# Attention without a division of the probabilities: the inverse sums go through memory and scale the values

## The chip, the core and the metric

The program runs on one core of a Trainium2 chip. Its engines work side by side, each through its own list in order: TensorE (PE in the profile, with PEld for its weight loads), VectorE (DVE), ScalarE (ACT), GpSimd (POOL) and SyncE (SP), which here only issues transfers. The metric is the device time of one execution in microseconds (us); lower is better.

## What is computed

A trunk of two layers over 512 positions of width 1024. Layer 0 mixes positions with a state-space scan and has a gated feed-forward part; layer 1 is attention over 16 heads, then a second feed-forward part. The change touches only the attention:

```python
s = jnp.einsum('bhqd,bhkd->bhqk', q_blk, k).astype(jnp.float32) * scale
s = jnp.where(key_pos[None, :] <= query_pos[:, None], s, NEG_INF)
p = jax.nn.softmax(s, axis=-1).astype(v.dtype)
return jnp.einsum('bhqk,bhkd->bhqd', p, v)
```

Each head has keys and queries of 96 and values of 64 numbers per position. The softmax divides each row of exp(s - max) by its sum; since that divisor belongs to a query, it can be applied to the row of probabilities, or later to the 64 values that come out for this query.

## The kernel before, in words

The kernel is written in a framework that takes the operations in program order, with their dependences and buffers, and works out by an estimate of its own the order of each engine's list. So an edit in one place can shift the order all around it. A tile name has a fixed number of buffers (`bufs`); who needs a buffer waits until its last reader is done.

Attention works on heads one by one (`for h in range(H)`), in four quarters of four heads. A quarter is opened (its three weight slabs are loaded by SP, split into a high part `wh` on ScalarE and a low part `wl` on VectorE, lines 141 and 142), its queries and keys are projected block by block, and it is closed (`close_q`, `close_k`): root mean squares by some 25 small VectorE operations (the tiles `r41...` and `r42...`), then the queries `Qt` and the keys `Kt` are scaled on VectorE and GpSimd. Quarters are projected ahead of their heads, so that three closings fall between the heads of earlier quarters.

For a head, `scores(h)` makes four blocks of rows of the score matrix in a PSUM bank (block i has 128 queries and (i + 1) * 128 keys), takes each row's negative maximum (line 968, VectorE), and makes `p = exp(s - max)` with its row sum `sm` on ScalarE (line 970). Line 971 inverts the sum on VectorE (one number per partition), and line 973 multiplies the block by it, on VectorE for block 3 and on GpSimd for blocks 0 to 2. `turn_p` transposes the blocks on TensorE into `pt` (line 982). For each pair of heads, `values` multiplies `pt` by the values `Vt` into one bank `ps_po` (line 1002): head h in partitions 0 to 63, head h + 1 in 64 to 127, the queries along the row. The bank is split into a high part `oh` (ScalarE, line 168) and a low part `ol` (VectorE, line 169), while the order of positions in the row is changed. Eight such pairs feed the output projection with the slabs `w_o`, three matmuls per product; one of its eight blocks of columns (`ps_w`) is worked into the attention from head 9 on, and parts of two more are placed among the last heads.

All transfers of the attention are issued by SP, one list in order: an issue that waits for a buffer or for data holds back all issues behind it.

Of the kernel before, what the change touches and what calls it, by code (L numbers as in the profile page):

```python
# [7 lines left out]
F32 = mybir.dt.float32  # L8
# [8 lines left out]
P = 128  # L17
D = 1024
S = 512
# [3 lines left out]
T = 4  # L23
# [55 lines left out]
def places(z):  # L79

    return z.rearrange("p (i c) -> p i c", i=T)


def by_place(z):

    return z.rearrange("p (c i) -> p i c", i=T)


class Trunk:
# [779 lines left out]
    def attention(self, low, krot, tabs, tf, tfs, maskb, identb):  # L869
        tc, nc, a = self.tc, self.nc, self.a  # L870
        v, g = nc.vector, nc.gpsimd
        M_, A_, S_ = ALU.mult, ALU.add, ALU.subtract
        ident = self.c("ident")

        def tt(out, x, y, op, eng=v):
            eng.tensor_tensor(out=out, in0=x, in1=y, op=op)

        qp = self.qp
        os = []
        quarters, heads, outs = {}, {}, {}  # L880
# [74 lines left out]
        def scores(h):  # L955
            qT, kT = heads[h, "q"], heads[h, "k"]
            mx = qp.tile([P, 4], F32, name="mx")
            sm = qp.tile([P, 4], F32, name="sm")
            pbs = [None] * 4
            b2 = self.ps("s")  # L960
            for i in (0, 2, 1, 3):
                n = (i + 1) * P
                bank = b2 if i in (0, 2) else self.ps("s")
                ps = bank[:, 384:512] if i == 0 else bank[:, 0:n]
                nc.tensor.matmul(out=ps, lhsT=qT[:, i * P:n], rhs=kT[:, 0:n], start=True, stop=False)  # L965
                nc.tensor.matmul(out=ps[:, i * P:n], lhsT=identb, rhs=maskb, start=False, stop=True)  # L966
                m1, s1 = mx[:, i:i + 1], sm[:, i:i + 1]
                v.reduce_max(out=m1, in_=ps, axis=AX.X, negate=True)  # L968
                pb = qp.tile([P, n], F32, name=f"p{i}")
                nc.scalar.activation(out=pb, in_=ps, func=AF.Exp, bias=m1, accum_out=s1)  # L970
                v.reciprocal(out=s1, in_=s1)  # L971
                eng = v if i == 3 else g
                eng.tensor_scalar(out=pb, in0=pb, scalar1=s1, scalar2=None, op0=M_)  # L973
                pbs[i] = pb
            heads[h, "p"] = pbs

        def turn_p(h, kbs, eng):
            bank = self.ps("a")
            at = 0
            for kb in kbs:  # L980
                for i in range(kb, 4):
                    nc.tensor.transpose(out=bank[:, at + (i - kb) * P:at + (i - kb + 1) * P], in_=heads[h, "p"][i][:, kb * P:(kb + 1) * P],
                                        identity=ident)
                at += S - kb * P
            pt = qp.tile([P, at], F32, name=f"pt{kbs[0]}", bufs=4)
            if eng is v:
                v.tensor_copy(out=pt, in_=bank[:, 0:at])
            else:
                nc.scalar.activation(out=pt, in_=bank[:, 0:at], func=AF.Copy)
            at = 0  # L990
            for kb in kbs:
                heads[h, "t", kb] = pt[:, at:at + S - kb * P]
                at += S - kb * P

        def values(h):

            Vt = quarters[h // 4][4]
            po = self.ps("po")
            with tc.high_priority():
                for kb in range(4):  # L1000
                    for e in (1, 0):
                        nc.tensor.matmul(out=po[64 * e:64 * e + 64, kb * P:], lhsT=Vt[:, kb, (h + e) % 4, :], rhs=heads[h + e, "t", kb],  # L1002
                                         start=kb == 0, stop=kb == 3)
            os.append(self.pair(h // 2, "o"))
            self.split(*[y.rearrange("p (i c) -> p c i", i=T) for y in os[-1]], po.rearrange("p (c i) -> p c i", i=T))

        open_quarter(0)
        for b in range(4):
# [9 lines left out]
        for h in range(2):  # L1018
            turn(h, "q")
            turn(h, "k")  # L1020
        scores(0)
        for h in range(H):
            nq, nb = divmod(h + 7, 4)
            if h + 1 < H:
                scores(h + 1)
# [13 lines left out]
            if h % 2 == 0 and h:  # L1039
                values(h - 2)  # L1040
# [9 lines left out]
            if nq < 4:  # L1050
                proj_kv(nq, nb)
                if nb == 3:
                    close_k(nq)
        values(H - 2)
        for m in range(KD):
            w, ps = early[m] if m < 1 else (self.weights(a["w_o"][m], (KD, P), pieces=2 if m in (3, 4) else 1), self.ps(("", "s", "s", "a", "a", "a", "s", "a")[m]))
# [102 lines left out]
```

## Time and profile before

| | |
|---|---|
| median of 3 runs | 1229.52 us (1227.26 to 1230.77) |
| the profiled execution, its own time | 1228.52 us |
| its span, first to last instruction | 1226.7 us |
| mean granted clock of TensorE | 0.979 of full speed |
| TensorE busy | 1182.0 us (96% of the span) |
| VectorE, ScalarE, GpSimd busy | 664.2, 489.2, 137.2 us |
| attention, heads and closings | about 680 to 835 us from the span's start |

A view of the profile gives, for engines or groups of instructions, the busy time, the count of instructions, the mean duration of one, and what ended the idle time before them. A busy TensorE is not TensorE at its peak: its matmuls overlap, and their ends are modelled. Times in timelines and windows count from the start of the span.

### The profile page before, as it was taken

What the parts mean: (1) busy time and instruction counts of PE and PEld (TensorE: products, weight loads), DVE (VectorE), ACT (ScalarE), POOL (GpSimd) and SP (SyncE); (2) the same over time, 40 slices, a digit from 0 to 9 for tenths busy, and PEclk for the clock granted to TensorE, in tenths of its full rate; (3) what the DMA queues carried; (4) which work ended last, traced back from release to release, by engine and by line L of the source; (5) the groups of instructions that cost most, each with busy time, mean ns of one, the idle gap of its engine ahead of it and who ended that gap; (6) DMA issues with size and microseconds to landing.
All of it is one profiled execution on the core that took longest, in us unless ns stands there. A gap on an engine that the chain in (4) does not pass through costs nothing.

```text
span 1226.7 us, 15533 instructions
## 1 busy us (share of the span) xinstructions
PE 1182.0 (96%) x6133; PEld 959.8 (78%) x6136; DVE 664.2 (54%) x1194; ACT 489.2 (40%) x821; POOL 137.2 (11%) x149
## 2 busy tenths in 40 slices
PE   7977999999999999999999898999999999999998
PEld 6766777888888888888878676667888888888887
DVE  7797894357444444333358767744844444443221
ACT  7646444254232232233245766644432332322110
POOL 0300000030000000000234445432100000000000
PEclk9978799999999999999999899999999999999999
DMA  6210012323333233333222101103233232333331
GB/s 230 69 27 27 28 36 86 103 86 104 91 98 103 92 97 99 95 95 95 86 88 67 37 2 41 52 2 103 86 103 103 87 103 91 99 99 103 120 114 46
DMA packets 31896, 100.96 MB, mean 82 GB/s; under 512 B 3664, under 2 KB 4688, under 8 KB 31824
## 3 DMA queue, kind: packets, MB, share of 16 engines
q1 hardware_dynamic: 31680, 99.97, 26.2%
q8 instruction: 48, 0.79, 0.3%
q14 instruction: 24, 0.20, 0.1%
q10 hardware_dynamic: 144, 0.00, 0.0%
HBM read 97.86 MB, written 2.10 MB: 81 GB/s over the span
## 4 chain that ended last, share of the span: by engine, by line
PE 83%; DVE 9%; ACT 4%; issue 2%; POOL 1%; DMA 1%; SPq 0%; DVEq 0%; ACTq 0%
PE ps_ps L155 20%; PE ps_ps L154 20%; PE ps_ps L153 19%; PE ps_s L965 2%; PE ps_x L153 2%; PE ps_x L155 2%; PE ps_x L154 2%; PE ps_a L153 2%; PE ps_a L154 2%; PE ps_a L155 2%; DVE wl L142 1%; PE ps_x L638 1%; PE ps_g L153 1%; PE ps_x L606 1%; PE ps_po L1002 1%
## 5 line engine op out<-in xcount | busy, mean ns | idle before, releaser
L141 ACT ACTIVATE wh<-w 128x1024 fp32r<-128x1024 f32 (+3 forms) x193 | 191.3, 993 | 548.0 <-PE ps_ps L154 351.0
L142 DVE TENSOR_TENSOR wl<-w,wh 128x1024 fp32r<-128x1024 f32 (+3 forms) x193 | 221.9, 1151 | 212.8 <-ACT wh L141 212.7
L153 PE MATMUL ps_ps<-fh,wh 128*128 128x512 f32 x704 | 274.2, 390 | 0.0
L155 PE MATMUL ps_ps<-fh,wl 128*128 128x512 f32 x704 | 273.4, 389 | 0.0
L154 PE MATMUL ps_ps<-fl,wh 128*128 128x512 f32 x704 | 273.4, 389 | 0.0
L154 PEld LDWEIGHTS ps_ps<-fl,wh 128*128 128x128 f32 x704 | 132.1, 188 | 28.1 <-issue 0.5
L153 PEld LDWEIGHTS ps_ps<-fh,wh 128*128 128x128 f32 x704 | 132.1, 188 | 27.6 <-issue 0.5
L155 PEld LDWEIGHTS ps_ps<-fh,wl 128*128 128x128 f32 x704 | 132.1, 188 | 27.5
L153 PE MATMUL ps_ps<-ah,wh 128*128 128x512 f32 x352 | 136.9, 389 | 0.0
L154 PE MATMUL ps_ps<-al,wh 128*128 128x512 f32 x352 | 136.9, 389 | 0.0
L155 PE MATMUL ps_ps<-ah,wl 128*128 128x512 f32 x352 | 136.9, 389 | 0.0
L743 DVE TENSOR_TENSOR ut<-ps_ps,rstd 128x512 f32<-128x512 f32 x44 | 30.4, 691 | 127.8 <-PE ps_ps L155 127.8
L263 POOL TENSOR_TENSOR acc<-acc,sq 128x512 f32<-128x512 f32 x21 | 30.5, 1452 | 564.6 <-ACT sq L258 316.0
L153 PEld LDWEIGHTS ps_ps<-ah,wh 128*128 128x128 f32 x352 | 66.1, 188 | 13.8
L154 PEld LDWEIGHTS ps_ps<-al,wh 128*128 128x128 f32 x352 | 66.1, 188 | 13.8
L155 PEld LDWEIGHTS ps_ps<-ah,wl 128*128 128x128 f32 x352 | 66.1, 188 | 13.5
L740 DVE TENSOR_TENSOR gt<-ps_ps,rstd 128x512 f32<-128x512 f32 x44 | 30.4, 691 | 83.2 <-PE ps_ps L155 83.1
L973 POOL TENSOR_SCALAR p<-p,sm 128x128 f32<-128x128 f32 (+2 forms) x48 | 45.8, 960 | 70.6 <-DVE sm L971 59.3
L965 PE MATMUL ps_s<-kT,qT 96*128 96x384 f32 (+3 forms) x128 | 46.6, 466 | 1.5 <-ACT p L970 1.5
L970 ACT ACTIVATE p<-ps_s,mx 128x128 f32<-128x128 f32 (+3 forms) x64 | 33.4, 525 | 22.8 <-DVE mx L968 18.6
L168 ACT ACTIVATE ah<-ut 128x512 fp32r<-128x512 f32 x44 | 27.9, 634 | 30.7 <-DVE ut L744 30.7
L968 DVE TENSOR_REDUCE mx<-ps_s 128x1 f32<-128x128 f32 (+3 forms) x64 | 30.8, 486 | 15.1 <-PE ps_s L966 14.6
(384 smaller groups left out, 1756.1 us busy)
## 6 DMA issues: line engine op xcount, KB each, us to landing
w<-w_gu SPq DMA_DIRECT2D x88, 512.0 KB, 3.5
w<-w_down SPq DMA_DIRECT2D x32, 512.0 KB, 3.5
w<-w_glu SPq DMA_DIRECT2D x12, 512.0 KB, 3.5
w<-w_down SPq DMA_DIRECT2D x16, 384.0 KB, 3.1
w<-w_in SPq DMA_DIRECT2D x7, 512.0 KB, 3.6
w<-w_o SPq DMA_DIRECT2D x6, 512.0 KB, 3.2
x<-xT SPq DMA_DIRECT2D x8, 256.0 KB, 6.0
bc<-ssm_bc SPq DMA_DIRECT2D x8, 256.0 KB, 2.8
```

What stands on the lines that cost most here:

```text
L141: nc.scalar.activation(out=wh[:, c], in_=w[:, c], func=AF.Copy)
L142: nc.vector.tensor_tensor(out=wl[:, c], in0=w[:, c], in1=wh[:, c].bitcast(F32), op=ALU.subtract)
L153: nc.tensor.matmul(out=out, lhsT=lh, rhs=rh, start=start, stop=False)
L154: nc.tensor.matmul(out=out, lhsT=lh, rhs=rl, start=False, stop=False)
L155: nc.tensor.matmul(out=out, lhsT=ll, rhs=rh, start=False, stop=stop)
L263: nc.gpsimd.tensor_tensor(out=acc, in0=acc, in1=sq, op=ALU.add)
L740: v.tensor_tensor(out=gt, in0=pss[0], in1=rstd, op=ALU.mult)
L743: v.tensor_tensor(out=ut, in0=pss[1], in1=rstd, op=ALU.mult)
L965: nc.tensor.matmul(out=ps, lhsT=qT[:, i * P:n], rhs=kT[:, 0:n], start=True, stop=False)
L968: v.reduce_max(out=m1, in_=ps, axis=AX.X, negate=True)
L970: nc.scalar.activation(out=pb, in_=ps, func=AF.Exp, bias=m1, accum_out=s1)
L973: eng.tensor_scalar(out=pb, in0=pb, scalar1=s1, scalar2=None, op0=M_)
```

## The change

Nothing is divided in `scores` any more: `p` stays exp(s - max). The eight sums of a pair of heads are collected in one tile of 128 x 8 and inverted by one instruction. They stand one query per partition, but are needed along the row, so SP writes them to memory as 4-byte elements in the transposed order (`row`, 2 x 4 x 128 numbers) and reads them back twice, each head's 512 numbers into 64 partitions (`inv`, 128 x 512). The values are multiplied by `inv` as they leave their bank, into a tile `o` that uses the two buffers of the squares (`sq`), with the change of order in this operation; `oh` and `ol` are then made from `o`.

```diff
+            if h % 2 == 0:
+                heads[h // 2, "s"] = qp.tile([P, 2, 4], F32, name="sm")
+            sm = heads[h // 2, "s"][:, h % 2]
...
                 nc.scalar.activation(out=pb, in_=ps, func=AF.Exp, bias=m1, accum_out=s1)
-                v.reciprocal(out=s1, in_=s1)
-                eng = v if i == 3 else g
-                eng.tensor_scalar(out=pb, in0=pb, scalar1=s1, scalar2=None, op0=M_)
                 pbs[i] = pb
             heads[h, "p"] = pbs
+            if h % 2:
+                inverse_sums(h // 2)
+
+        def inverse_sums(j):
+            sm = heads.pop((j, "s"))
+            v.reciprocal(out=sm, in_=sm)
+            row = tc.dram_tile([2, 4, P], F32, name=f"row{j}")
+            nc.sync.dma_start(out=row.rearrange("e i p -> p e i"), in_=sm, allow_slow_non_contiguous=True)
+            inv = qp.tile([P, S], F32, name="inv")
+            for e in range(2):
+                nc.sync.dma_start(out=inv[64 * e:64 * e + 64], in_=row[e:e + 1].rearrange("e i p -> e (i p)").broadcast_to([64, S]))
+            heads[j, "inv"] = inv
...
+            o = self.hp.tile([P, S], F32, name="o", tag="sq", bufs=2)
+            tt(places(o), by_place(po), by_place(heads.pop((h // 2, "inv"))), M_)
             os.append(self.pair(h // 2, "o"))
-            self.split(*[y.rearrange("p (i c) -> p c i", i=T) for y in os[-1]], po.rearrange("p (c i) -> p c i", i=T))
+            self.split(*os[-1], o)
```

The lists of the engines show where this lands. On SP, before, between the opening of the last quarter (`w_kv_b`, then two pieces of `w_q_b`) and the first slabs of the output projection (numbers behind names tell one tile from another):

```order
L134 DMA w_6277<-w_kv_b 128x1024
L134 DMA w_6283<-w_q_b 128x768
L134 DMA w_6289<-w_q_b 128x384
L134 DMA w_6745<-w_o 128x1024
L134 DMA w_7164<-w_o 128x1024
L134 DMA w_7196<-w_o 128x1024
```

The same place of SP's list in the changed kernel, up to the third slab of `w_o`:

```order
L983 DMA row0_5622<-sm_5571 128x8x1
L986 DMA inv_5624<-row0_5622 64x512 x2
L134 DMA w_6248<-w_q_b 128x768
L983 DMA row1_5867<-sm_5735 128x8x1
L986 DMA inv_5869<-row1_5867 64x512 x2
L983 DMA row2_6057<-sm_5948 128x8x1
L986 DMA inv_6059<-row2_6057 64x512 x2
L134 DMA w_6254<-w_q_b 128x384
L134 DMA w_6692<-w_o 128x1024
L134 DMA w_7094<-w_o 128x1024
L983 DMA row3_6317<-sm_6185 128x8x1
L986 DMA inv_6319<-row3_6317 64x512 x2
```

Three pairs' round trips now stand ahead of the last piece of `w_q_b`, and each holds SP until its write has landed. VectorE in the third closing, before (`ol4` is pair 4, heads 8 and 9; `r42...` and `r41...` belong to the closing of the last quarter):

```order
L187 SCALAR_TENSOR_TENSOR sc2_6617<-r42t_6620,r42y_6621 128x32
L187 SCALAR_TENSOR_TENSOR sc1_6661<-r41t_6664,r41y_6665 128x16
L169 TENSOR_TENSOR ol4_6840<-ps_po_6830,oh4_6839 128x128x4
L876 TENSOR_TENSOR sc2_6617<-sc2_6617,tf_5055 128x32
L876 TENSOR_TENSOR sc1_6661<-sc1_6661,tf_5055 128x16
```

VectorE in the changed kernel where pair 4's scaled values `o_6783` wait for `inv_6509`; its reciprocal (`sm_6398`) stands 20 rows ahead of `o`:

```order
L970 TENSOR_REDUCE mx_6634<-ps_s_6636 128x1
L876 TENSOR_TENSOR ss_6263<-ss_6263,tfs_5056 128x16
L182 TENSOR_SCALAR r42y_6574<-r42x_6572 128x32
L181 TENSOR_SCALAR r41x_6618<-ss_6263 128x16
L185 TENSOR_TENSOR r42t_6573<-r42y_6574,r42x_6572 128x32
L876 TENSOR_TENSOR o_6783<-ps_po_6774,inv_6509 128x512
L182 TENSOR_SCALAR r41y_6620<-r41x_6618 128x16
L186 SCALAR_TENSOR_TENSOR r42t_6573<-r42t_6573,r42y_6574 128x32
```

What waited only for a bank and ScalarE behind the closing's last small operations now stands among the first of them, and waits for a transfer as well. The last place is the end of the list: VectorE in the changed kernel from the last maximum of heads 12 and 13 (`mx_6850`) to their scaled values (`o_7047`, which needs `inv_6877`, made from the reciprocal in the second row):

```order
L970 TENSOR_REDUCE mx_6850<-ps_s_6851 128x1
L970 TENSOR_REDUCE mx_6931<-ps_s_6950 128x1
L981 RECIPROCAL sm_6793<-sm_6793 128x8
L970 TENSOR_REDUCE mx_6931<-ps_s_6933 128x1
L999 COPY pt2_6966<-ps_a_6963 128x256
L999 COPY pt0_6987<-ps_a_6982 128x512
L970 TENSOR_REDUCE mx_6989<-ps_s_7001 128x1
L970 TENSOR_REDUCE mx_6989<-ps_s_7007 128x1
L970 TENSOR_REDUCE mx_6931<-ps_s_6933 128x1
L876 TENSOR_TENSOR o_7047<-ps_po_7038,inv_6877 128x512
```

In the kernel before, a head's reciprocals and block 3's multiplication stood among such rows, and nothing in them waited for a transfer.

## Rows read from the trace of the kernel before

**Rows 1.** The page, busy time of an engine, share of the span, instructions

```profile
PE 1182.0 (96%) x6133; PEld 959.8 (78%) x6136; DVE 664.2 (54%) x1194; ACT 489.2 (40%) x821; POOL 137.2 (11%) x149
```

**Rows 2.** Windows: stretch, its length, busy us of each engine (instructions), clock, DMA

```profile
840.00:860.00 20.00, 20.00 (x90) 16.57 (x89) 9.16 (x10) 8.57 (x11) 6.47 (x5) 1.00 0.40 133
...
680.00:835.00 155.00, 143.88 (x800) 101.92 (x799) 104.28 (x320) 95.15 (x230) 64.86 (x65) 0.97 0.08 26
```

**Rows 3.** Waits of TensorE, 675 to 870 us: total, times, longest

```profile
PE ps_a L950 <- POOL Qt L876: 2.4, 2, 1.3
...
PE ps_a L982 <- POOL p L973: 0.3, 1, 0.3
```

**Rows 4.** Groups by line, 675 to 870 us: busy us, mean ns | idle before

```profile
L973 POOL TENSOR_SCALAR p<-p,sm 128x128 f32<-128x128 f32 (+2 forms) x48 | 45.8, 960 | 70.6 <-DVE sm L971 59.3 <-DVE r42y L187 2.3 <-DVE sc L187 2.2
L970 ACT ACTIVATE p<-ps_s,mx 128x128 f32<-128x128 f32 (+3 forms) x64 | 33.4, 525 | 22.8 <-DVE mx L968 18.6 <-DVE ss L876 2.6 <-issue 0.7
L968 DVE TENSOR_REDUCE mx<-ps_s 128x1 f32<-128x128 f32 (+3 forms) x64 | 30.8, 486 | 15.1 <-PE ps_s L966 14.6
...
L971 DVE RECIPROCAL sm<-sm 128x1 f32<-128x1 f32 x64 | 9.6, 156 | 8.5 <-ACT p L970 8.2
...
L169 DVE TENSOR_TENSOR ol<-ps_po,oh 128x512 fp32r<-128x512 f32 x8 | 8.5, 1065 | 10.2 <-ACT oh L168 10.2
...
L973 DVE TENSOR_SCALAR p<-p,sm 128x512 f32<-128x512 f32 x16 | 8.4, 526 | 0.3
```

**Rows 5.** Windows of the three closings, their sum (690:710, 728:750, 769:787)

```profile
sum 60.00, PE 55.54 PEld 40.00 DVE 55.28 ACT 40.48 POOL 23.90; mean PE 18.51 PEld 13.33 DVE 18.43 ACT 13.49 POOL 7.97
```

**Rows 6.** The same windows, VectorE's instructions on tile sm alone

```profile
sum 60.00, DVE 6.46; mean DVE 2.15
```

**Rows 7.** Groups by line elsewhere: the same operations without a change of order

```profile
L169 DVE TENSOR_TENSOR al<-ut,ah 128x512 fp32r<-128x512 f32 x44 | 30.2, 686 | 2.1 <-ACT ah L168 2.1
...
L743 DVE TENSOR_TENSOR ut<-ps_ps,rstd 128x512 f32<-128x512 f32 x44 | 30.4, 691 | 127.8 <-PE ps_ps L155 127.8
```

**Rows 8.** Timelines of VectorE and GpSimd: start us, duration us, instruction

```profile
744.29 2.32 POOL L973 TENSOR_SCALAR p<-p,sm 128x384 f32<-128x384 f32 x2 [1.44 <-DVE sm L971]
...
744.37 0.55 DVE L185 TENSOR_TENSOR r42t<-r42y,r42x 128x32 f32<-128x32 f32 x1
744.84 0.17 DVE L185 TENSOR_TENSOR r41t<-r41y,r41x 128x16 f32<-128x16 f32 x1
...
672.12 1.90 POOL L876 TENSOR_TENSOR Kt<-Kt,sc 128x1024 f32<-128x1024 f32 x1 [2.36 <-DVE sc L876]
...
672.22 1.85 DVE L187 SCALAR_TENSOR_TENSOR r42y<-r42t,r42y 128x32 f32<-128x32 f32 x1
```

**Rows 9.** The chain that ended last, in order of time, 680 to 835 us

```profile
790.67 2.16 POOL p L973 x2
```

**Rows 10.** DMA issues of the page and the full list: KB each, us to landing

```profile
out<-x SPq DMA_DIRECT2D x7, 256.0 KB, 2.0
...
w<-w_o SPq DMA_DIRECT2D x4, 256.0 KB, 3.3
...
w<-w_kr_a SPq DMA_DIRECT2D x1, 128.0 KB, 2.1
...
pos<-positions ACTq DMA_DIRECT2D x1, 2.0 KB, 1.6
```

**Rows 11.** Windows around that 2 KB load (issued at 189.7 us), last columns DMA

```profile
190.70:191.00 0.30, 0.30 (x5) 0.20 (x2) 0.30 (x1) 0.00 (x0) 0.00 (x0) 1.00 0.23 7
```

**Rows 12.** TensorE's timeline among the last heads

```profile
799.25 2.38 PE L1002 MATMUL ps_po<-pt,Vt 128*64 128x512 f32 x16
...
802.21 1.07 PE L965 MATMUL ps_s<-kT,qT 96*128 96x512 f32 x2
...
803.18 0.71 PE L982 MATMUL ps_a<-ctab,p 128*128 128x128 f32 x5
803.73 0.81 PE L965 MATMUL ps_s<-kT,qT 96*128 96x384 f32 x2
```

More of the change, by code (lines that the diff above doesn't have):

```diff
@@ L957, in scores @@
             mx = qp.tile([P, 4], F32, name="mx")
-            sm = qp.tile([P, 4], F32, name="sm")
+            if h % 2 == 0:
+                heads[h // 2, "s"] = qp.tile([P, 2, 4], F32, name="sm")
+            sm = heads[h // 2, "s"][:, h % 2]
             pbs = [None] * 4
```

## The prediction

> **What bounds the kernel now.** I read the page first, for the engine that the whole span waits for: TensorE is busy for 96% of it [rows 1], so an edit elsewhere is worth something only where TensorE stands still. Then the windows, for the stretch that the change touches: from 680 to 835 us, the heads and the closings of three quarters, TensorE is busy for 143.88 of 155 us and VectorE for 104.28 [rows 2]. That leaves 155 - 143.88 = 11.1 us of plain idle time, the most that this stretch can give back unless matmuls also run closer together. After 840 us TensorE is busy without a gap, 90 matmuls in 20 us, 0.22 us for each [rows 2]; what comes earlier there ends earlier.
>
> Then the waits, for what TensorE waits for. The removed multiplication is named directly once, for 0.3 us; the largest row, 2.4 us, is the scaling of the queries on GpSimd at a closing [rows 3], which stands at the end of a long run of VectorE work. So I looked at the closings: in their three windows of 60 us together VectorE is busy for 55.28 [rows 5]. There VectorE sets the pace, between them it does not. The gain must come from the closings, and an operation that waits on VectorE there hurts most.
>
> **What is removed.** 64 reciprocals of 156 ns (9.6 us), 16 multiplications on VectorE of 526 ns (8.4 us), 48 on GpSimd of 960 ns (45.8 us) [rows 4]. GpSimd only waits for VectorE most of the time [rows 4], so its 45.8 us are no gain as such. Of the 18 us on VectorE, 6.46 lie in the closings [rows 6]; the others lie where VectorE has time, and count for nothing. Their cover is the idle time of VectorE between the closings; without it they would be worth 11.5 us more.
>
> **What is added on VectorE.** Eight reciprocals of 128 x 8: nothing of that form is in the trace; it lies between one of 128 x 1 (156 ns) and a 128 x 512 operation (526 ns) [rows 4], and nearer to the first; 0.16 us. Eight multiplications `o`. From a bank, 128 x 512 in order took 691 ns [rows 7]; with a change of order, `ol` took 1065 ns [rows 4]. `o` changes the order and reads two tiles so: 1.07 us. `ol` then runs in order from memory on the chip, like `al`: 686 ns [rows 7], 0.38 us less. So a closing with one pair in it gets 0.16 + 1.07 - 0.38 = 0.85 us more; three get 2.6. Net in the closings: 6.46 - 2.6 = **3.9 us**.
>
> **What GpSimd's work costs VectorE.** While two multiplications of `p` ran on GpSimd from 744.29 us on, a small operation with two inputs took 0.55 us, and its like right behind it 0.17; at 672.22 another took 1.85 us, as long as GpSimd's scaling of `Kt` beside it, 1.90 [rows 8]. Without `p` on GpSimd the first kind goes away: 0.38 us each; I count one for each closing, **1.0 us** in all (bounds 0 and twice that). But `ol`, which read a bank and one tile, now reads two tiles on the chip like these operations. At pair 2 the new list has it right behind the scales that start GpSimd's two scalings, so it can be held there, by up to 1.9 us; TensorE waits for those scalings then anyway [rows 3], so I count nothing and keep 1.9 for the range. The Trainium skill, SBUF — State Buffer, section Who interferes with whom, has it so: a VectorE instruction with two inputs in SBUF and a GpSimd instruction that reads SBUF shut each other out for the whole instruction, and one with a single such input is free. By that rule the gain and the loss are both real; the trace agrees, 1.85 beside 1.90 us.
>
> **One place on the chain.** At 790.67 us two multiplications on GpSimd, 2.16 us, lie on the chain that ended last [rows 9]. They go, but the transposes behind them still need the transposed queries and the exponentials: I take half, **1.0 us**.
>
> **The trip through memory.** The sums of a pair are written as 1024 elements of 4 bytes and read back as 2 x 128 KB in rows of 2 KB. The nearest row for many small pieces is the load of 2 KB as 128 pieces of 16 bytes: 1.6 us to landing [rows 10], of which its transfers filled a window of 0.3 us [rows 11]. With eight times the pieces, if only that part grows, 1.3 + 8 x 0.3 = 3.7 us; if nothing grows, 1.6; if all grows, 8 x 1.6 = 12.8. A write of 256 KB lands in 2.0 us [rows 10], so the direction alone is not dear. I take 3.7, since the row shows the rest as waiting. The reads: 128 KB land in 2.1 us, 256 KB in 2.0 to 3.3 [rows 10]; I take 2.6 for the two. With the reciprocal, 0.2 + 3.7 + 2.6 = **6.5 us** from the last sum to `inv`.
>
> The Trainium skill, DMA: Bandwidth & Descriptors, section Rules for kernel authors, warns of just this form: a last dimension with gaps becomes one descriptor per element. From its sections on one DMA's anatomy (about 2 us fixed) and on bandwidth (about 10.5 ns per small packet, 64 of them on an engine here) I estimate 2.7 us for the write; by that the sum below would be 1.0 us better. No row of before shows a write of 4-byte pieces.
>
> What covers the 6.5 us? Only the distance in the lists between a pair's reciprocal and its `o`. VectorE's rows in the attention take 104.28 / 320 = 0.33 us on average [rows 2]. *Pairs 0, 1 and 3* have 23 rows or more between, with waits among them: over 7.5 us, hidden. *Pair 4*: 19 rows in the third closing, 6 us. Its write is also issued right behind a half slab of `w_o`, which takes 3.3 us to land [rows 10] and goes first, so I add 1 us (bounds 0 and 3.3): 7.5 - 6 = 1.5 us late. The whole closing stands behind that `o` on VectorE, and the last four heads wait for the closing: **-1.5 us**. *Pair 6*: from the last score of head 13 to the end of pair 6's values TensorE's new list holds 19 transposes (0.11 each, five in 0.55), four scores (0.97 for the widest, in proportion 2.44 for all), three projection matmuls (0.22) and the values (2.38) [rows 2, 12], together 7.6 us. The reciprocal ends 0.49 + 0.53 + 0.16 us and about 0.5 of hand-overs after that score [rows 4], 1.7 us: cover 5.9, late by 0.6. But until TensorE needs pair 6 it has nine transposes, 15 projection matmuls and a narrow score to do, 4.5 us, and `o` with its two parts takes 1.07 + 2 x 0.69: 2.1 us are to spare, no cost. *Pair 7*: behind its last score TensorE first waits for the exponentials, as VectorE's reciprocal does; then come transposes (the last six after the wait, 0.7), 21 projection matmuls and the values, 0.7 + 4.6 + 2.4 = 7.7 us: hidden by 1.2.
>
> On SP, three trips stand ahead of the last piece of `w_q_b`, and each holds SP until its write has landed. Behind *pair 2's* VectorE has 14 rows, two of them low parts of slabs at 1.1 us and one an `o`, to the one that needs the piece: 2.2 + 1.07 + 11 x 0.33 = 6.9 us; 0.2 + 3.7 for the write, 2.6 for the piece and 0.5 for its high part make 7.0: just covered. GpSimd's list issues no transfers.
>
> **The sum.** 3.9 + 1.0 + 1.0 - 1.5 = 4.4 us less than the profiled execution's own 1228.5 us: 1224.1. The median of the three runs is 1.0 us above that execution, but the runs spread over 3.5; I leave the number at **1224 us**.
>
> **The rivals.** *Nothing comes of it.* TensorE could be held in the closings by the order of its own list and by ScalarE (40.48 of 60 us busy [rows 5]), so that only the wait that names `p` goes, 0.3 us [rows 3]: 1228 us. For it speaks that TensorE is busy for 55.54 of these 60 us [rows 5]; against it that this busy time includes overlapping ends. *More comes.* If the shorter way from exp to transpose, and a GpSimd that is free at once, close all idle time, 11.1 us [rows 2] go: 1217 us. Speaks against it that most waits are for work that stays. *The trip is slow* (the other side): the write takes w us instead of 3.7. Pair 4 is then late by w - 2.2, the piece behind pair 2 by w - 3.6, pair 6 costs w - 5.2 and pair 7 w - 4.9, when positive. At w = 5.5 that is 3.3 + 1.9 + 0.3 + 0.6 = 6.1 us, about the whole gain of 5.9; that is the point from which it decides. At 8 it is 16.1, so 1228.5 - 5.9 + 16.1 = 1239 us; at 12.8, 35.3 us or 1258. For it speaks that no row shows such a write; against it the short window of the small load [rows 11].
>
> **How the numbers follow.** Under 0.3%, 3.7 us, a measurement of this kernel can't tell a change from none. The forecast (its own range 1221 to 1227) has 0.44, nothing 0.22, more 0.14, the slow trip 0.20. Faster by over 0.3%: 0.30 of the forecast and the 0.14, so 0.44; within: 0.14 of the forecast, 0.18 of nothing, 0.02 of the slow trip, so 0.34; slower: 0.18 of the slow trip and 0.04 of nothing, for an order of the lists that happens to be worse, so 0.22. The range takes in "more" with some closer matmuls, 1215, and the slow trip up to w = 7.4, 1236.
>
> **What would show it.** VectorE's busy time in the attention falls by about 64 x 0.156 + 16 x 0.526 - 8 x 0.85 = 11 us; GpSimd's by 46; the closings are shorter by one to two us each; `row` lands after 3 to 4.5 us and `inv` after about 2.5. The forecast is wrong if `o` waits for a transfer by more than 2 us at any pair but 4, if `row` takes over 5.5 us, or if the closings keep their length although VectorE has less to do.

## The result, and the profile after

| | before | changed kernel |
|---|---|---|
| median of four runs | 1228.76 us (1227.26 to 1230.77) | 1261.62 us (1259.93 to 1267.39) |
| ratio to before | 1 | 1.028 (95% interval 1.026 to 1.030) |
| span of the profiled run | 1226.7 us | 1260.2 us |
| mean granted clock of TensorE | 0.979 | 0.969 |
| GpSimd busy | 137.2 us | 88.8 us |

The change costs 32.9 us, where 4.4 us of gain were forecast and 1236 us was the end of the range. The first thing to read is the time that SP needed for the two kinds of new transfers. The list of DMA issues of the changed kernel (KB each, median us from issue to landing) and the waits of SP's own list (total, times, longest):

```profile
inv<-row SPq DMA_DIRECT2D x16, 128.0 KB, 3.8
...
row<-sm SPq DMA_DIRECT2D x8, 4.0 KB, 9.8
...
SPq L986 <- DMA row<-sm: 72.9, 8, 10.2
```

The write of 4 KB lands after 9.8 us; the forecast took 3.7, from the load of 128 small pieces [rows 10, 11]. SP stands still for 72.9 us behind the eight writes. The next view is the chain that ended last in the changed kernel (start us, us, what), around the first and the last pair and the three between them that count:

```profile
695.18 9.62 DMA row<-sm
...
705.38 5.68 DMA inv<-row
...
733.57 9.92 DMA row<-sm
...
744.65 3.63 DMA w<-w_q_b
...
786.07 10.85 DMA row<-sm
...
797.43 3.06 DMA inv<-row
...
827.41 8.48 DMA row<-sm
...
849.75 8.69 DMA row<-sm
...
858.95 4.26 DMA inv<-row
```

Five of the eight writes lie on the chain: those of pairs 0, 2, 4, 6 and 7. At pair 2 it is not `o` that waits but the piece of `w_q_b` behind the trip, as in the forecast's worry. In the kernel before, the chain had a 2.16 us scaling of `p` on it [rows 9]; that one is gone. Where `o` itself waits stands in VectorE's timeline (in brackets: idle us before it, and for what):

```profile
711.18 1.05 DVE L876 TENSOR_TENSOR o<-ps_po,inv 128x512 f32<-128x512 f32 x1 [3.11 <-DMA inv<-row]
...
800.61 1.05 DVE L876 TENSOR_TENSOR o<-ps_po,inv 128x512 f32<-128x512 f32 x1 [7.89 <-DMA inv<-row]
...
840.75 1.05 DVE L876 TENSOR_TENSOR o<-ps_po,inv 128x512 f32<-128x512 f32 x1 [8.65 <-DMA inv<-row]
...
863.33 1.05 DVE L876 TENSOR_TENSOR o<-ps_po,inv 128x512 f32<-128x512 f32 x1 [12.08 <-DMA inv<-row]
```

Are the transfer engines busy in these ten microseconds? The windows around pair 2's write, which was issued at 733.57 and landed at 743.5 (the last two columns are the busy share of the 16 transfer engines and GB/s):

```profile
734.30:735.30 1.00, 1.00 (x10) 0.99 (x9) 0.38 (x1) 1.00 (x2) 0.00 (x0) 1.00 0.47 4
735.30:743.40 8.10, 6.40 (x35) 4.50 (x33) 6.01 (x13) 3.08 (x8) 1.27 (x2) 1.00 0.03 1
```

The 1024 pieces pass within about one microsecond; then 8 us go by in which the engines do nearly nothing, and only after these is the transfer reported as landed. The forecast's w was a time of passing plus a fixed wait of 1.3 us; the real one is nearly all wait. The Trainium skill, DMA: Bandwidth & Descriptors, section Anatomy of one DMA, says of transfers issued by GpSimd that their end is signalled only when the last byte is confirmed in the memory that it goes to, and that this is most of a fixed cost of about 2 us. These windows, of a transfer issued by SP, agree in kind, with 8 us in place of its 2.

### The profile page after: what moved, and what is told of

The parts are those of the page before. It is cut to its first block, busy times and chain, and to the rows that moved or that the text cites. A ratio compares the mean times of both kernels' runs of the same rounds, so it can differ in the third digit from the quotient of the medians.

```text
span 1260.2 us, 15473 instructions
## 1 busy us (share of the span) xinstructions
PE 1188.4 (94%) x6136; PEld 961.3 (76%) x6136; DVE 659.7 (52%) x1130; ACT 484.3 (38%) x821; POOL 88.8 (7%) x101
## 3 DMA queue, kind: packets, MB, share of 16 engines
q1 hardware_dynamic: 41280, 102.10, 26.7%
## 4 chain that ended last, share of the span: by engine, by line
PE 81%; DVE 7%; DMA 6%; ACT 4%; issue 1%; POOL 1%; SPq 0%; DVEq 0%; ACTq 0%
PE ps_ps L155 19%; PE ps_ps L154 19%; PE ps_ps L153 19%; DMA row<-sm 4%; PE ps_s L967 2%; PE ps_x L153 2%; PE ps_x L155 2%; PE ps_a L153 2%; PE ps_x L154 2%; PE ps_a L154 2%; PE ps_a L155 2%; DMA inv<-row 1%; PE ps_x L638 1%; PE ps_a L950 1%; PE ps_g L153 1%
## 5 line engine op out<-in xcount | busy, mean ns | idle before, releaser
L142 DVE TENSOR_TENSOR wl<-w,wh 128x1024 fp32r<-128x1024 f32 (+3 forms) x193 | 225.4, 1169 | 218.9 <-ACT wh L141 218.8
L153 PE MATMUL ps_x<-zh,wh 128*128 128x512 f32 x96 | 37.5, 392 | 0.7 <-ACT wh L141 0.7
```

The lines of the kernel that those rows point to most:

```text
L142: nc.vector.tensor_tensor(out=wl[:, c], in0=w[:, c], in1=wh[:, c].bitcast(F32), op=ALU.subtract)
L153: nc.tensor.matmul(out=out, lhsT=lh, rhs=rh, start=start, stop=False)
```

## The experiments

Twelve kernels. First the trip was taken away, then its wait, then its form; four kernels measured transfers alone.

**No trip.** What is the rest of the change worth?

```diff
-            row = tc.dram_tile([2, 4, P], F32, name=f"row{j}")
...
-            heads[j, "inv"] = inv
...
-            tt(places(o), by_place(po), by_place(heads.pop((h // 2, "inv"))), M_)
+            tt(places(o), by_place(po), by_place(self.x[:, 0]), M_)
```

> The changed kernel without the write and the two reads; the values are multiplied by a tile of x in place of inv, so the division is left out. Theory of the wait: the whole loss is the trip, and what the forecast counted as gain is there without it: 1228.5 - 5.9 = 1222.6, so 1220 to 1226. Theory of the lists: the new order and the extra pass over the values are worse by themselves: over 1240.

1225.05 us, ratio 0.997 (0.9955 to 0.998) to before: the new lists and the extra pass over the values are not worse, they save 3.7 us. The theory of the lists falls. (Here, in the next kernel and in the one with spaced elements the computing engines have the changed kernel's lists in the attention, row for row.)

**All transfers, but nobody waits for `inv`.** Only the last two lines of the diff above; SP's list too is that of the changed kernel.

> The changed kernel with all its transfers, issued in the same order, but the values are multiplied by a tile of x in place of inv, so nothing on VectorE waits for inv (the division is left out). Theory of the wait (o stands and waits for inv): only the piece of w_q_b behind the third trip is still late, some 10 us at most, so 1228 to 1236. Theory of the queue (SyncE is held by each write, and the slabs behind come late): 1250 or more.

1236.92 us (ratio 1.007, 1.005 to 1.008), just above the first theory's range. So the loss against the run without a trip splits: 1236.92 - 1225.05 = 11.9 us are there although nobody waits for `inv`, and 1261.6 - 1236.9 = 24.7 us come when `o` waits too. ScalarE's wait for the piece of `w_q_b` is there in both kernels, here (first line) and in the changed one:

```profile
742.60 0.52 ACT L141 ACTIVATE wh<-w 128x384 fp32r<-128x384 f32 x1 [9.63 <-DMA w<-w_q_b]
```

```profile
748.30 0.52 ACT L141 ACTIVATE wh<-w 128x384 fp32r<-128x384 f32 x1 [9.92 <-DMA w<-w_q_b]
```

Against the run without a trip, `o` is 0.3 us early at pair 1 and 8.5 us late at pair 2, behind this piece, for whose high part TensorE waits 6.6 us. At pair 4 it is 11.5 us late: there the matmuls of the values take 4.13 us in place of 2.37, at a granted clock of 0.54 from 785 to 790 us. So most of the 11.9 us is the late piece, and some 3 us are not a late slab alone.

**Transfers by themselves.**

```python
...
d = tc.dram_tile([8, P], F32, name=f"rowa{r}")
nc.sync.dma_start(out=d.rearrange("e p -> p e"), in_=src[:, :, 0], **slow)
...
```

> A kernel that computes nothing: twelve forms of transfer, three times each, every one issued by SyncE with nothing else in flight, and the next only when it has landed. It leaves all of the reference out. Measured is the time from issue to landing. The write of 1024 elements of 4 bytes took 9.8 us in the changed kernel. Theory of the pieces: the time grows with the number of pieces, whatever their address; then 1024 pieces take 8 to 10 us alone, 512 take 5 to 6, 128 take 2 to 3; 1024 pieces that lie 64 bytes apart, or are 64 bytes long, or are read instead of written, also take 8 to 10. Theory of shared lines: pieces that many partitions write into the same 64 bytes of memory hold each other up; then the 1024 pieces 64 bytes apart take under 4 us, and so do 1024 pieces of 64 bytes and the 1024 pieces that are read. Theory of small writes: any write under 64 bytes is slow in memory; then the pieces 64 bytes apart are as slow as the packed ones, pieces of 64 bytes are fast, and reads are fast. Theory of contention: alone, the write takes 2 to 4 us as forecast, and 9.8 comes from the transfers beside it. Eight rows of 512 bytes should take about 2 us in all four.

SP's waits behind them (total, times, longest; each line is the transfer that the next issue waited for). Such a wait begins when the issue is over, so it is some 0.2 to 0.8 us shorter than the time from issue to landing:

```profile
SPq L1159 <- DMA rowb<-src: 22.7, 3, 7.8
SPq L1159 <- DMA rowc<-src: 21.7, 3, 7.5
SPq L1159 <- DMA rowa<-src: 17.3, 2, 9.2
SPq L1159 <- DMA rowk<-src: 16.5, 3, 5.7
...
SPq L1159 <- DMA rowd<-src: 7.3, 3, 2.5
...
SPq L1159 <- DMA rowi<-src: 5.3, 3, 1.8
...
SPq L1159 <- DMA rowe<-src: 3.2, 3, 1.1
```

`rowa` is the kernel's write, 1024 packed elements; `rowb` has 512 and `rowc` 128 of them and they hardly take less (7.6 and 7.2 us each, total over times). `rowd` is 1024 elements 64 bytes apart: 2.4 us. `rowi`, 1024 pieces of 64 bytes, 1.8; `rowk`, 8 bytes apart, 5.5; `rowe`, 128 pieces of 32 bytes, 1.1. So the theories of the pieces and of small writes fall: the price is in small elements written close to each other. Contention falls with the next run, which took each transfer quite alone; here other small transfers were under way beside `rowa` and `rowb`.

**Spacing.** The same with 4 to 128 bytes between 1024 elements, and with fewer packed elements.

> A kernel that computes nothing, again transfers by themselves, each issued when the one before has landed, three times: 1024 elements of 4 bytes written with 4, 8, 16, 32, 64 and 128 bytes from one to the next; then 1, 16, 128 and 512 elements packed; 128 elements to memory on the chip; 8 rows of 512 bytes; 1024 elements read; the two reads of 64 x 512. If elements in the same 64 bytes wait for each other, what counts is how many share them: packed 9 to 10 us, 8 bytes apart 5.5 to 6.5, 16 bytes 4 to 4.5, 32 bytes about 3.3, 64 and 128 bytes 2.9, and 16 packed elements alone already take 7 or more. If lines are 32 bytes, it is flat from 32 bytes on. If instead every element costs alike and only the gaps help a little, 16 elements take under 2.5 us. To memory on the chip: under 2.5 us if the sharing is a matter of the memory off the chip, 7 or more if of the transfer engines.

```profile
SPq L1154 <- DMA gap4b<-src: 31.7, 3, 10.9
SPq L1154 <- DMA few512b<-src: 25.0, 3, 8.4
SPq L1154 <- DMA few128b<-src: 21.8, 3, 7.6
SPq L1154 <- DMA gap8b<-src: 12.6, 3, 4.4
...
SPq L1154 <- DMA gap16b<-src: 7.9, 3, 2.8
...
SPq L1154 <- DMA gap64b<-src: 7.0, 3, 2.6
...
SPq L1198 <- DVE src L1157: 6.0, 3, 2.0
...
SPq L1154 <- DMA few16b<-src: 2.8, 3, 1.0
SPq L1154 <- DMA long<-src: 2.7, 3, 0.9
SPq L1154 <- DMA few1b<-src: 2.4, 3, 0.8
```

Packed 10.6 us (31.7 / 3), 8 bytes apart 4.2, 16 bytes 2.6, and from there on flat at 2.3 to 2.5. Eight rows of 512 bytes (`long`), the same 4 KB, 0.9. The simple form of my theory falls as well: 16 packed elements, which fill 64 bytes as fully as the 1024 do, wait 0.9 us, as one element does (0.8). The line of L1198 stands for 128 packed elements written to memory on the chip: with a VectorE step behind the write, SP waits 2.0 us each time, where the same elements written off the chip take 7.3. By the expectation's own rule the price is a matter of the memory off the chip, not of the transfer engines. The read of 1024 elements holds SP for 1.8 us.

**Which closeness counts?** Groups of different size and distance.

> A kernel that computes nothing, transfers by themselves as before: 32, 64 and 128 elements of 4 bytes packed into one row; 128 elements as 8 groups of 16 that lie 512 bytes apart, and 256 bytes apart; as 4 groups of 32 and as 2 groups of 64, 512 bytes apart; 128 packed elements that come from one partition; 128 elements 128 bytes apart. The run before left 16 packed elements at 1.3 us and 128 at 7.7, so sharing 64 bytes can't be all. If elements that fall into the same 512 bytes are taken one after another, some 0.05 us each: 32 take 2 to 3 us, 64 take 4 to 4.7, 128 take 7.7, 8 groups of 16 under 2, 8 groups of 16 at 256 bytes 2 to 3, 4 groups of 32 the same, 2 groups of 64 again 4 to 4.7. If the unit is 64 bytes, all the groups take as long as 128 packed, 7 to 8; if it is 256 bytes, 64 packed take as long as 128. From one partition: as long as from 128 if the place in memory counts, under 2 us if the many partitions do.

```profile
SPq L1154 <- DMA one128b<-src: 20.9, 3, 7.3
...
SPq L1154 <- DMA one64b<-src: 19.2, 3, 6.6
SPq L1154 <- DMA alone128b<-src: 18.4, 3, 6.3
...
SPq L1154 <- DMA four32b<-src: 9.3, 3, 3.2
SPq L1154 <- DMA one32b<-src: 8.4, 3, 2.9
...
SPq L1154 <- DMA eight16b<-src: 3.8, 3, 1.7
SPq L1154 <- DMA apart128b<-src: 3.1, 3, 1.1
```

Per transfer: 32 packed 2.8, 64 packed 6.4, 128 packed 7.0; 128 as 4 groups of 32, 512 bytes apart, take 3.1, as 8 groups of 16 1.3, all apart 1.0. From one partition it is the same (6.1). A unit of 512 bytes falls, since 64 take nearly as long as 128. A last run of this kind used 1024 elements from one partition:

> A kernel that computes nothing, transfers by themselves as before, all of 4-byte elements that come from one partition: 1024 packed; 1024 in groups of 16 (64 bytes) that begin 128, 256 and 512 bytes apart; groups of 8 and of 4 at every 64 bytes; groups of 2 at every 16 bytes; groups of 32 at every 512 bytes; 256 in groups of 16 at every 256 bytes. The rule of 512 bytes that I expected fell in the runs before: 64 packed took as long as 128, and four transfers of groups of 32 took 7.4 us in the kernel. If what counts is how many elements share 64 bytes, once there are many in all: groups of 16 take 8 to 11 us at any distance, groups of 8 some 5 to 6, of 4 some 3, pairs at 16 bytes (8 in 64 bytes) 5 to 6. If it is how many share 256 bytes: groups of 16 at 128 bytes take 7 or more, at 256 and 512 bytes 3 to 5, groups of 4 at 64 bytes (16 in 256) as those. If distance is what helps, 512 bytes beat 256, and 256 beat 128.

Packed 10.6 us again (31.9 / 3), every grouped form of 1024 between 5.8 and 7.6. It decides nothing between the units: taken from one partition, the packets themselves pass slowly (the transfer engines have a busy share of 0.10 over the window of 4.6 us behind a packed issue, and 0.00 over the next 4.9 us, until it lands), so this run can't tell the forms apart. What is shown is that 1024 packed elements wait 10.6 us whether they come from 128 partitions or from one.

**The changed kernel with spaced elements.** One transfer fills `rows`, a [16, 4, P, 16] tile, in advance; the sums are written 64 bytes apart, and `inv` is read from 2 KB of which only every sixteenth number is a sum, so the division is left out in effect.

```diff
+        rows = tc.dram_tile([16, 4, P, 16], F32, name="rows")
...
-            row = tc.dram_tile([2, 4, P], F32, name=f"row{j}")
-            nc.sync.dma_start(out=row.rearrange("e i p -> p e i"), in_=sm, allow_slow_non_contiguous=True)
+            row = rows[2 * j:2 * j + 2]
+            nc.sync.dma_start(out=row[:, :, :, 0].rearrange("e i p -> p e i"), in_=sm, allow_slow_non_contiguous=True)
...
```

> The changed kernel, with the lists of all computing engines as they were: the inverse sums are written with 64 bytes from one to the next, and inv is read from the first 2 KB of each head's stretch, which was filled once in advance, so that most of the divisors are wrong numbers (the division is left out in effect). If the shared 64 bytes are the whole cause, row lands after 3 us, the trip takes 0.2 + 3 + 3.9 = 7 us, about what the forecast had, and the time is 1223 to 1232. If in the kernel the write is slow for another reason as well, or the reads alone are enough to stop the closings, over 1240.

```profile
rows<-sm SPq DMA_DIRECT2D x8, 4.0 KB, 2.9
```

1229.83 us, ratio 1.001 (1.000 to 1.0025): 31.8 us of the 32.9 are gone with the place of the elements alone. The write lands after 2.9 us in place of 9.8, the reads behind it after 3.0 in place of 3.8. So the place of the elements in memory is the cause of nearly all of the loss; why packed ones land so late stays open.

**Groups of 32, with the division.** The row begins each 32 elements at a new 512 bytes; four writes of 32 partitions each, 8 groups of 32 elements in every one.

```diff
...
+            for b in range(4):
+                nc.sync.dma_start(out=row[:, :, b, 0:32].rearrange("e i q -> q e i"), in_=sm[32 * b:32 * b + 32], allow_slow_non_contiguous=True)
...
```

> The changed kernel with the division and nearly the same lists: the row is laid out with 32 elements at the start of each 512 bytes, written by four transfers of 32 partitions each, and read in pieces of 128 bytes. If 128 elements in the same 512 bytes were the price, the writes land in 3 to 3.5 us, the reads in 3 to 4, and the time is that of the spaced run, 1227 to 1234. If reading in small pieces or four writes for one takes back what is won: 1240 to 1255.

1264.06 us (ratio 1.029, 1.026 to 1.032). My expectation missed, and the issue list says why:

```profile
inv<-row SPq DMA_DIRECT2D x16, 128.0 KB, 3.7
row<-sm SPq DMA_DIRECT2D x32, 1.0 KB, 7.4
```

Each of the four lands after 7.4 us, though 4 groups of 32 alone had taken 3.1; these have 8 groups each and are issued one behind the other. So the reads in small pieces are not the matter (3.7 against 3.8 us), and where the write is slow again, the time is the changed kernel's again.

**GpSimd as the issuer**, once with the changed kernel's form and once with the groups of 32 (`nc.gpsimd.dma_start` for `row` and `inv`).

> The changed kernel with the write and the reads issued by GpSimd in place of SyncE, so that no slab of weights stands behind them; GpSimd's scalings of queries and keys now do. If the part of the loss that unread showed (1236.9 - 1225.1 = 11.8 us) is SyncE being held, it goes and the wait of o stays: 1250. If GpSimd, held for 10 us by each write, delays the scalings as SyncE delayed the slabs, 1256 to 1275.

> The run before, issued by GpSimd in place of SyncE (the order on the other engines shifts with it). With SyncE the trip of the fifth pair stands between two slabs of w_o. If that, and not the trip's own length, is what is left over the time without a trip (1229.8 - 1225.1 = 4.8 us in the spaced run): 1224 to 1228. If GpSimd's scalings, or the trip itself, are: 1229 to 1242.

1264.68 us (ratio 1.030), in the range for a GpSimd that is held, and 1253.46 us (ratio 1.021), above both ranges. Who issues does not change the landing (9.2 and 8.3 us). In the first, GpSimd is held for 61.9 us by seven of the writes, as SP was. In the second, whose lists differ, 10.6 us are saved against the groups issued by SP; which part is the queue and which the order wasn't separated.

**Rows of 512 bytes, by a transpose on TensorE.** Two versions with the division. The first takes a bank of its own for the transposed sums and inverts them there:

```diff
-            v.reciprocal(out=sm, in_=sm)
+            ps = self.ps("a")
+            nc.tensor.transpose(out=ps[0:8, 0:P], in_=sm.rearrange("p e i -> p (e i)"), identity=ident)
...
+            v.reciprocal(out=inv[0:8, 0:P], in_=ps[0:8, 0:P])
...
```

> The changed kernel, but TensorE transposes the eight sums of a pair first, the reciprocal is taken of the transposed 8 x 128, and the write has 8 rows of 512 bytes; the reads stay. If the form of the write is the price: it lands in 2 to 3 us, the trip takes about 7 us in place of 14, and the time is 1222 to 1232. If any write that is read back at once takes this long, or the time is lost by the reads and the order: 1250 or more.

1239.86 us (ratio 1.009, 1.008 to 1.011), between the two ranges. The write is quick now: SP waits 9.8 us for eight of them together (`SPq L988 <- DMA row<-inv: 9.8, 8, 2.0`), and the reads land in 3.0. But the reciprocal of 8 x 128 takes 0.94 us on VectorE where 128 x 8 took 0.19, and TensorE's list has a transpose that stands behind the last exponential, for 2.25 us at the first pair. What part each of these has in the 15 us over the run without a trip stays open.

The second transposes after the reciprocal, in the free part of the bank of the first turned block, and lets ScalarE copy:

> A version with the division: the inverse sums are transposed on TensorE in the same bank as the first block of probabilities, copied by ScalarE, written as 8 rows of 512 bytes and read as before. Trip about 0.3 + 0.3 + 1.5 + 3 = 5 us, and VectorE's added reciprocal over 8 x 128 of the run before is not there. If the waits are what counts: 1224 to 1231. If the transposes in TensorE's list and the other order cost as much as in the run before, 1236 to 1242.

1230.86 us, ratio 1.0025 (1.001 to 1.004). Within the expectation, and no gain over before: no version here that keeps the division beats it.

## Why the prediction was wrong

**The step that failed** is the price of the write: "With eight times the pieces, if only that part grows, 1.3 + 8 x 0.3 = 3.7 us ... I take 3.7, since the row shows the rest as waiting." It measured 9.8, inside the bounds of 1.6 and 12.8 that were kept. The row was a load of 16-byte pieces into the chip. It shows how long many pieces take to pass, and passing was indeed short here (one microsecond). It can't show the wait behind that, which took the other 8 us when the elements lay packed off the chip. The prediction's second estimate, 2.7 us, fell short in the same way; both lie nearer to the spaced form, which lands in 2.9. Two of the prediction's own signs of being wrong are in the result: `row` took over 5.5 us, and `o` waited for `inv` by 3.1, 8.7 and 12.1 us at pairs 0, 6 and 7.

**The rival that came true** is the slow trip, with its mechanism, its places and its sign; it had 0.20, and the range ended at w = 7.4. Its formula gives at w = 9.8: pair 4 late by 7.6, the piece behind pair 2 by 6.2, pair 6 by 4.6, pair 7 by 4.9, in all 23.3, so 1228.5 - 5.9 + 23.3 = 1246 us, 16 us under the measured time. The lists of the changed and of the spaced kernel are the same in the attention, so the start of each `o` in their timelines gives the price pair by pair (us later than in the spaced kernel, where pair 0 starts at 707.38 and pair 4 at 780.88):

| pair | 0 | 1 | 2 | 3 | 4 | 5 | 6 | 7 |
|---|---|---|---|---|---|---|---|---|
| later by | 3.8 | 5.4 | 13.6 | 13.6 | 19.7 | 18.9 | 25.8 | 31.3 |

The steps are 8.1 at pair 2, 6.2 at pair 4, 6.9 at pair 6 and 5.5 at pair 7. The four places are the forecast's, and their sizes near its own (27 against 23). What the formula left out is pair 0, 5.4 us by the time of pair 1. With the 4.8 us by which the spaced kernel is behind the one without a trip, these make up the loss: 4.8 + 5.4 + 26.7 = 36.9 us, where 1261.6 - 1225.1 = 36.6 were measured. "*Pairs 0, 1 and 3* ... hidden" was right for a trip of 6.5 us, but the rival kept their cover as if it had no end. At pair 0 the reciprocal starts at 694.7 and VectorE is ready for `o` at 708.1: 13.4 us of cover, for a trip of 16.5.

**The reads** took 3.8 us in place of 2.6 (the `inv` of pair 0, beside a piece of `w_q_b`, 5.7), about one microsecond more wherever `o` waits for `inv`; in the spaced kernel they took 3.0.

**The gain** was over-sized: 5.9 us forecast without the lateness, 3.7 measured (no trip, interval 2.5 to 5.5 by the ratio). VectorE's own terms were right: `o` 1063 ns (1.07 forecast), `ol` 684 (686), the reciprocal of 128 x 8 195 (160). The closings did get shorter: from its first `r42x` to its scaling of `Qt` VectorE took 6.9, 6.0 and 7.2 us before and 4.3, 6.2 and 5.4 without a trip, 4.1 us less in all, where 3.9 + 1.0 were forecast. How much of this reached the end isn't shown, because the granted clock differs too: over the stretch from 680 to 835 us it was 0.97 before and 1.00 without a trip, and no term of the forecast has that.

**Had the write taken 3.7 us, the forecast of a gain would still have failed.** The spaced kernel has a trip of the length that was forecast, and takes 1229.8 us, not 1224.1. Of the terms it is pair 4's lateness, "7.5 - 6 = 1.5 us late": `o` waits for `inv` for 2.05 us there, about as forecast, and starts 2.1 us later than without a trip, but the next `o` is 5.8 us later (803.44 and 797.65), and so are the last two. The place where this grows is TensorE's wait for the closing behind pair 4's `o`. First the spaced kernel's timeline and its window, then the same in the kernel without a trip:

```profile
787.34 1.92 PE L950 MATMUL ps_a<-ctab,Qt 128*96 128x128 f32 x8 [3.23 <-DVE Qt L876]
...
785.00:797.00 12.00, 8.79 (x36) 7.35 (x37) 4.13 (x9) 5.66 (x13) 2.95 (x2) 0.57 0.10 22
```

```profile
785.21 1.05 PE L950 MATMUL ps_a<-ctab,Qt 128*96 128x128 f32 x8 [1.40 <-DVE Qt L876]
...
785.00:797.00 12.00, 10.91 (x71) 7.51 (x73) 5.94 (x15) 8.07 (x21) 1.90 (x1) 1.00 0.00 1
```

A wait of 3.23 us in place of 1.40, and then eight matmuls take 1.92 us in place of 1.05, at a granted clock of 0.57 over the 12 us in place of 1.00 (0.50 is the lower of its two levels, 1.2 GHz): about half of the matmuls get done (36 and 71). In the spaced kernel TensorE stood still from 784.1 to 787.3 us, and the granted clock was 1.00 up to 786, 0.50 from 787 to 796 and 1.00 again from 797; without a trip it stood still from 783.8 to 785.2, and the clock stayed at 1.00. In the changed kernel the same shows more often; its granted clock is 0.62 in the 9 us around each of the last two `o`:

```profile
840.00:849.00 9.00, 6.16 (x15) 4.19 (x15) 3.43 (x6) 1.76 (x5) 0.00 (x0) 0.62 0.00 0
861.00:870.00 9.00, 4.90 (x14) 3.90 (x15) 3.94 (x6) 3.42 (x7) 0.00 (x0) 0.62 0.10 29
```

So a microsecond of lateness was worth more than a microsecond here. That the forecast counted each at its own length is its second error; the 3.7 us between 2.1 and 5.8 are the size of it at this place. That the lower clock, and not the order of the work, makes all of the difference was read, not tried.

**What was right**: that the closings get shorter and the gain is small, that GpSimd's 46 us are no gain as such, that SP is held by each write and `w_q_b` behind pair 2 suffers, and the four places that turn late when the write is slow.

## What to carry to other kernels

A small transfer's price is its landing, and the landing of a write depends on where its elements fall in memory: 1024 four-byte elements packed into 4 KB landed in 10 us, the same elements 16 bytes or more apart in about 3, and 4 KB as eight rows in 1.2. A price taken from a load did not hold for this write; where no row shows the form, the sum needs the far bound, and every cover, the long ones too, has to be held against that bound. And before a detour off the chip is put on a chain that TensorE waits for, the gain without the detour should be known: here 3.7 us, which even a good trip used up.

## What the runs showed of the hardware that was not expected

- Packed 4-byte writes to memory wait long after their packets have passed: 64 elements 6.4 us, 128 7.0, 512 8.3, 1024 10.6; 16 elements 0.9 and 32 2.8. It does not follow the number of elements alone (1024 of them 16 bytes apart: 2.6), nor whether 64 bytes are filled (16 elements: 0.9), nor the source (one partition or 128). To memory on the chip 128 packed elements took at most 2.0.
- After a short packed write is reported as landed, the next access can still be slow: the read of one element behind the 16 packed ones took longer than the same read behind spaced ones. SP's timeline in the spacing run (issue to the next issue):

```profile
117.03 0.24 SPq L1154 DMA_DIRECT2D rb<-gap64b  x1
118.78 0.36 SPq L1180 DMA_DIRECT2D gap128b<-src  x1
...
127.49 0.21 SPq L1154 DMA_DIRECT2D rb<-few16b  x1
130.85 0.35 SPq L1189 DMA_DIRECT2D few128b<-src  x1
```

  1.75 us behind the spaced write, 3.36 behind the 16 packed elements, and 2.9 to 3.7 behind 128 and 512 packed ones; but behind 1024 packed ones it is 1.8 to 2.2 again. Whether the memory was still at work on the write isn't shown. What rule of the memory makes all these numbers stays open: groups of 32 alone took 3.1 us for 128 elements, and 7.4 in the kernel for 256 at a time.
